# A gated hybrid layer on one core: the modulation vectors computed from unsplit fp32 weights in two column groups of TensorE

## The chip, the cores and the metric

The kernel runs on one core of a Trainium2 chip. A core has TensorE (PE, matrix products and transposes into PSUM), VectorE (DVE), ScalarE (ACT), GpSimd (POOL), and SyncE (SP), whose queue issues all DMA transfers of this kernel. The metric is the device time of one execution in microseconds; the median of three runs of the kernel before is 1617.76 us (1617.69 to 1618.45).

## The reference

The layer takes 1024 latent tokens and 256 context tokens of width 1024. Each token is RMS-normalised and modulated, and the result is multiplied by a large input matrix `w_in`; two branches (a gated linear attention, GLA, and a differential attention) follow, then gates, an output projection and a residual. The part that matters here is the modulation:

```python
mod_x = jax.nn.silu(c) @ w_ada[layer] + b_ada[layer]
mod_c = jax.nn.silu(c_ctx) @ w_ada[layer] + b_ada[layer]
sh_x, sc_x, g_x = jnp.split(mod_x[:, None, :], 3, axis=-1)
sh_c, sc_c, g_c = jnp.split(mod_c, 3, axis=-1)
pl = project(modulate(x, sh_x, sc_x), w_in[layer])      # rms_norm(x) * (1 + scale) + shift
pc = project(modulate(ctx, sh_c, sc_c), w_in[layer])
```

So two vectors (latent and context) of 1024 are multiplied by the first 2048 columns of `w_ada` (8 MB in fp32) before any token can be modulated. The third part, `g_x`, is needed only where `w_out` is prepared. Everything is fp32, and the results must keep fp32 accuracy.

## The kernel before

A large product is made of three fp32r products: each operand is split into a high part (a ScalarE copy into fp32r) and a low part (a VectorE subtraction), and `mm3` issues high by high, high by low and low by high. One such product of 128 x 128 by 128 x 512 is one TensorE record in the trace.

The kernel writes out the order of work on PE, ScalarE, VectorE and GpSimd itself. Tasks are Python generators; `Driver` (line 59) keeps a modelled clock for each engine, and a task that yields is taken up again at the modelled time at which its data are there, the lowest `prio` first. `At(70.0)` is a modelled time of that clock. What is emitted first stands first in the engine's queue, and the engines take their queues in order, so an instruction whose data are late holds up all behind it. Tiles come from pools with fixed numbers of slots (`TAGS`, line 235 on; `w` has 18, `p` 5, `pl` 4, `raw` 3, `l5` 3, `x2` 5, `x4` 1, `g5` 6; the PSUM banks are `mm` 3, `tp` 2, `gs`, `go`, `gt` 1 each); `acq` waits for a free slot, `rel` gives it back.

The first stretch is `prologue` (line 505). `consts` loads the two vectors, makes their SiLU and transposes them into the columns `col`. `loads` (532) then issues the transfers: for each of eight blocks `k` of 128 rows the first half of the modulation weights (512 columns of shift and 512 of scale, two tiles of `w`), between them the first four token tiles (`XL`, line 680, says behind which block), then two blocks of `w_in`, then the second half. Token tiles are normalised by `xnorm`.

`ada(part)` (583) makes the products of a half. In the first half it is plain fp32: the two columns of `col` are the stationary operand, 512 columns of weights stream past, and shift and scale go to the banks `gs` and `go`. In the second half the weights go into `raw` and `l5` slots, `conv` (566) splits them into high and low parts in slots of `w` and `pl`, and the products are fp32r: four stationary columns (`cs`: high and low of both vectors) against the high weights and two against the low ones. At the end of a half ScalarE copies one bank and VectorE the other into SBUF, eight small transposes bring them into columns (bank `gt`), and VectorE adds the bias: `shsc[part]`, the shift and scale of four of the eight row blocks of tokens. `ev_sh[part]` says that they are there.

The end of `prologue` transposes the tokens: for each of the eight row blocks four transposes into a `tp` bank, and `hblock` (640) applies shift and scale on ScalarE, makes the high part on GpSimd and the low part on VectorE. The loop waits for `ev_sh` before it transposes a block.

`wstream` (686) loads and splits the blocks of `w_in`. Its first two transfers (`RAWS`) may go behind the first half, the others behind the second; the split of the later ones waits for the event `ev_wc`, which `conv` sets at its end, as do the token tiles 4 to 9. `job` (741) makes the products of one group of weights, for one group of output blocks after the other: the first group has `G0` = 3 blocks in the three `mm` banks (3 blocks x 8 k x 3 products), the next ones a single block. For the first weights, the GLA keys, `post_gk` copies the result out and releases `mm`.

`job_gate` (762) computes `g_x` on VectorE from the rest of `w_ada`: eight transfers of 512 KB, one after the other through the one slot `x4`, two operations each, a PE product with ones per half, and at the end the event `ev_gbt`. It is started at the modelled time 70. The pair weights (943) use `x4` too, and `presums` (1045) needs `ev_gbt` to prepare `w_out`; the GLA stage opens (`to_gla`, 1277) when `presums` has ended.

Of the kernel before, what the change touches and what calls it, by code (L numbers as in the profile page):

```python
# [232 lines left out]
class Hybrid:  # L233
# [27 lines left out]
    def __init__(self, tc, nc, a, out):  # L261
        self.tc, self.nc, self.a, self.out = tc, nc, a, out
        self.n, self.ny, self.ng, self.ys = 0, 0, 0, {}
        self.d = d = Driver()
        self.act, self.dve, self.pool = Engine(d, "ACT", nc.scalar), Engine(d, "DVE", nc.vector), Engine(d, "POOL", nc.gpsimd)
        self.free, self.freed = {}, {}
        self.pools = {}
        self.recent = []

# [78 lines left out]
    def mm(self, out, lhsT, rhs, start, stop, more=False):  # L348
        self.ins = self.nc.tensor.matmul(out, lhsT, rhs, start=start, stop=stop, skip_group_check=more).ins  # L349
# [76 lines left out]
    def consts(self):  # L426
# [78 lines left out]
    def prologue(self):  # L505
# [21 lines left out]
        ev_w = {(k, part): Event() for k in range(NK) for part in range(2)}  # L527
        ev_r = [Event() for _ in range(NK)]
        ev_sh = [Event(), Event()]
        shsc = [self.c(f"shsc{x}", [P, 2, 4, 2]) for x in range(2)]  # L530

        def loads():

            for part in range(2):
                for k in range(NK):
# [23 lines left out]
            d.set(self.ev_wl[1])  # L559
            yield self.ev_wc  # L560
            for i in range(4, 10):
# [3 lines left out]

        def conv():
            for k in range(NK):
                yield ev_r[k]
                tg, raw = ev_r[k].raw
                ev, tw = ev_w[k, 1], ("w", "pl")[k % 2]  # L570
                yield from self.acq(tw, 4)
                ev.w = []
                for s in range(2):
                    hi = self.t(tw, [P, 512], F32R)
                    lo = self.t(tw, [P, 512], F32R)
                    yield self.act.activation(hi, raw[:, s], AF.Copy)
                    e = (self.pool if s in self.CP else self.dve).tensor_tensor(lo, raw[:, s], hi.bitcast(F32), ALU.subtract)
                    ev.w.append((hi, lo))
                self.rel(tg, e)
                d.set(ev, e)  # L580
            d.set(self.ev_wc)

        def ada(part):


            m = 4 if part else 2
            pa = []
            for tg in ("gs", "go"):
                yield from self.acq(tg)
                pa.append(self.t(tg, [m, 512]))  # L590
            for k in range(NK):
                yield ev_w[k, part]
                for x, w in enumerate(ev_w[k, part].w):
                    if part:

                        prods = [(pa[x], self.cs[:, k], w[0]), (pa[x][:2], self.cs[:, k, :2], w[1])][::-1 if k else 1]
                        for y, (o, c, ww) in enumerate(prods):
                            e = self.mm(o, c, ww, k == 0 and y == 0, k == NK - 1 and y == 1)
                    else:
                        e = self.mm(pa[x], self.col[:, k:k + 9:8], w, k == 0, k == NK - 1)  # L600
                        self.rel("w", e)
                        yield AtPE(0)
                if part:
                    self.rel(("w", "pl")[k % 2], e, 4)
                    yield AtPE(0)
            md = []
            for x, tg in enumerate(("gs", "go")):
                yield from self.acq("p")
                md.append(self.t("p", [m, 512]))
                if x:  # L610
                    e = self.dve.tensor_copy(md[x], pa[x])
                else:
                    e = self.act.activation(md[x], pa[x], AF.Copy)
                self.rel(tg, e)
            if part == 0:
                d.spawn(ada(1), prio=-1)
            yield from self.acq("gt")
            pt = self.t("gt", [P, 2, 4, m])
            for x in range(2):
                yield d.whenpe(md[x])  # L620
                for y in range(4):
                    e = self.tr(pt[:, x, y], md[x][:, y * P:(y + 1) * P])
                self.rel("p", e)
            yield self.d.when(pt)
            ss = shsc[part]
            for x in range(2):
                o = 24 + 8 * x + 4 * part
                e = self.dve.scalar_tensor_tensor(ss[:, x], pt[:, x, :, 0:2], float(x), self.col[
                    :, o:o + 4].unsqueeze(2).to_broadcast([P, 4, 2]), ALU.add, ALU.add)
            if part:  # L630
                e = self.dve.tensor_tensor(ss, ss, pt[:, :, :, 2:4], ALU.add)
            self.rel("gt", e)
            d.set(ev_sh[part], e)

        yield from self.consts()
        self.d.spawn(loads(), prio=-2)
        self.d.spawn(conv(), prio=-2)
# [28 lines left out]
        for half in (0, 1, 2):  # L666
# [3 lines left out]
            for k in range(NK):  # L670
                yield ev_sh[k // 4]
                yield from self.acq("tp")
# [6 lines left out]

    XL = ({1: (0,), 2: (1,), 4: (2,), 6: (3,)}, {})  # L680
    RAWS = 2
    CP = ()
    G0, NG = 3, 2


    def wstream(self, jobs, tag, gate=None, prio=3, after=()):

        queue = [(n, src, c0, kk) for n, (src, c0) in enumerate(jobs) for kk in range(NK // 2)]
        wd = Weights({(n, k): Event() for n in range(len(jobs)) for k in range(NK)})
        loaded = [Event() for _ in queue]  # L690

        def load():
            for ev in after[:1]:
                yield ev
            for x, (n, src, c0, kk) in enumerate(queue):
                if gate and x in (0, self.RAWS):
# [4 lines left out]
                self.d.set(loaded[x], self.dma(raw, src[kk * 256:(kk + 1) * 256, c0:c0 + 512].rearrange(  # L701
                    "(k p) c -> p k c", p=P)))

        def run():
            for ev in after[1:]:
                yield ev
            for x, (n, src, c0, kk) in enumerate(queue):
                yield loaded[x]
                if gate and x == self.RAWS:
                    yield gate[2]  # L710
# [30 lines left out]
    def job(self, wd, n, items, width, mms, post, wtag, ptag="mm", first=1, last=2):  # L741

        gs = self.groups(items, first, last)
# [86 lines left out]
    def phase_a(self):  # L830
# [35 lines left out]

        self.ev_wl, self.ev_wc = [Event() for _ in range(2)], Event()
        wd = self.wstream([(self.win, j[0]) for j in jobs], "w", (*self.ev_wl, self.ev_wc))
        self.wload = wd.loaded
        self.ev_pl, self.ev_pw, self.ev_zl = Event(), Event(), Event()  # L870
# [538 lines left out]
    def post_gk(self, s, half, pm):  # L1409
        o, n = self.hspan(half)  # L1410
        yield from self.acq("p")
        st = self.t("p", [P, n])
        self.rel("mm", self.act.activation(st, pm, AF.Copy))
        self.store([(self.d_k[s][:, o:o + n], st)], ("p", 1))
# [1396 lines left out]
```

## Time and profile before

| | before |
|---|---|
| median of three runs | 1617.76 us |
| span of the profiled execution | 1614.1 us |
| PE busy | 1591.4 us (99%) |
| VectorE, ScalarE, GpSimd busy | 1224.4, 835.7, 634.3 us |
| first `w_in` product on PE | 27.90 us |
| granted TensorE clock | 1.00 in all slices |

The time of the profiled execution itself is not given; its span, from the first to the last instruction, is 3.66 us shorter than the median of the timed runs, and what lies around the span is in the timed runs only. In a row of a view, L349 is the helper that issues all matmuls, L375 the one for transposes, L201 the one for all work on ScalarE, VectorE and GpSimd, L314 the one for transfers; so groups are told apart by tiles (`out<-in`). `PEld` are weight loads, which overlap with matmuls. The modelled ends of matmuls overlap too; the spacing of their starts is what they cost in a row. Times in views are us from the start of the span.

### The profile page before, as it was taken

The numbers are of one execution on the slowest core, as the hardware profiler recorded it, in microseconds if no ns is written. First come the engines' busy times: TensorE is split into PE (matmuls) and PEld (weight loads), VectorE is DVE, ScalarE is ACT, GpSimd is POOL, SyncE is SP. The second block draws the span as 40 slices with busy tenths as digits, with TensorE's granted clock in tenths as the row PEclk, the third lists the DMA queues.
The fourth block names the chain that finished last, engine by engine and source line by source line (L and its number), as shares of the span: only waits on it lengthen the run. The fifth ranks groups of instructions, "written<-read, shape, count | busy, mean of one in ns | idle before, by whom it ended". The sixth has DMA issues, their size and how long they took to land.

```text
span 1614.1 us, 24349 instructions
## 1 busy us (share of the span) xinstructions
PE 1591.4 (99%) x8229; PEld 1328.1 (82%) x8229; DVE 1224.4 (76%) x2118; ACT 835.7 (52%) x1720; POOL 634.3 (39%) x663
## 2 busy tenths in 40 slices
PE   8999999999999999999999999999999999999999
PEld 3788888888888888888888788888888888888887
DVE  4787945676777779767677688878778888888994
ACT  4776523435343454555535566665665666656331
POOL 1500000001415667535564256656765666560000
PEclk9999999999999999999999999999999999999999
DMA  8576996998878367564645944545587545347662
GB/s 305 201 257 239 329 304 232 344 331 295 278 238 281 116 194 235 167 212 118 189 118 158 253 121 121 151 129 151 150 264 218 159 137 150 111 155 285 204 206 100
DMA packets 259565, 331.16 MB, mean 205 GB/s; under 512 B 22600, under 2 KB 160752, under 8 KB 259440
## 3 DMA queue, kind: packets, MB, share of 16 engines
q1 hardware_dynamic: 259440, 329.60, 63.8%
q8 instruction: 65, 1.06, 0.3%
q14 instruction: 60, 0.49, 0.1%
HBM read 225.20 MB, written 104.33 MB: 204 GB/s over the span
## 4 chain that ended last, share of the span: by engine, by line
PE 89%; DVE 4%; issue 2%; DMA 2%; ACT 1%; POOL 1%; SPq 0%; ACTq 0%; DVEq 0%; POOLq 0%
PE mm L349 30%; PE mb L349 11%; PE s L349 8%; PE mc L349 7%; PE b L349 6%; PE tp L349 5%; PE gt L349 5%; PE b L375 5%; PE go L349 4%; PE gs L349 4%; PE mz L349 2%; PE tp L375 2%; DVE sm L201 1%; POOL at L201 1%; DMA w<-in_w_ada 1%
## 5 line engine op out<-in xcount | busy, mean ns | idle before, releaser
L349 PE MATMUL mm<-w,h 128*128 128x512 f32 x912 | 231.0, 400 | 0.0
L349 PE MATMUL mb<-h,wt 128*128 128x512 f32 x840 | 223.0, 400 | 0.0
L201 DVE TENSOR_REDUCE sm<-s 128x1 f32<-128x1024 f32 (+1 forms) x192 | 193.3, 1037 | 10.7 <-PE s L349 6.6
L201 ACT ACTIVATE e<-s,sm 128x1280 f32<-128x1280 f32 x128 | 169.3, 1329 | 54.4 <-DVE sm L201 51.2
L349 PEld LDWEIGHTS mm<-w,h 128*128 128x128 f32 x912 | 167.4, 188 | 32.8
L201 POOL TENSOR_TENSOR at<-ac,at 128x512 fp32r<-128x512 f32 x128 | 188.2, 1471 | 10.7
L349 PEld LDWEIGHTS mb<-h,wt 128*128 128x128 f32 x840 | 151.4, 188 | 28.6 <-DVE ft L201 0.3
L201 POOL TENSOR_SCALAR at<-ac 128x512 fp32r<-128x512 f32 x128 | 96.9, 757 | 191.0 <-ACT ac L201 190.7
L349 PE MATMUL s<-hk,aq 128*128 128x512 f32 x744 | 169.0, 363 | 1.9 <-ACT e L201 1.8
L349 PE MATMUL mm<-h,w 128*128 128x512 f32 x672 | 168.2, 400 | 1.0 <-DVE h L201 1.0
L349 PEld LDWEIGHTS mm<-h,w 128*128 128x128 f32 x672 | 123.7, 188 | 26.4 <-DVE h L201 1.5
L201 DVE TENSOR_TENSOR w<-raw,w 128x512 fp32r<-128x512 f32 x128 | 96.0, 766 | 54.2 <-ACT w L201 52.0
L349 PEld LDWEIGHTS s<-hk,aq 128*128 128x128 f32 x744 | 117.7, 189 | 18.5 <-ACT e L201 3.6
L349 PE MATMUL b<-at,vv 128*128 128x256 f32 x960 | 130.1, 287 | 1.1 <-ACT ac L201 0.8
L349 PEld LDWEIGHTS b<-at,vv 128*128 128x128 f32 x960 | 119.5, 191 | 2.8 <-ACT ac L201 1.0
L201 ACT ACTIVATE w<-raw 128x512 fp32r<-128x512 f32 x128 | 78.1, 626 | 84.2 <-PE tp L349 23.8
L201 ACT ACTIVATE ac<-b 128x512 f32<-128x512 f32 x122 | 72.5, 598 | 91.8 <-PE b L375 91.7
L201 POOL TENSOR_TENSOR sm<-sm,nhalf 128x2 f32<-128x2 f32 (+2 forms) x94 | 107.7, 1146 | 27.9 <-DVE sm L201 22.7
L201 DVE SCALAR_TENSOR_TENSOR e<-e,sm,e 128x1280 f32<-128x1280 f32 x64 | 117.9, 1842 | 1.0
L349 PE MATMUL mm<-w,g 128*128 128x512 f32 x432 | 105.7, 389 | 0.0
L349 PEld LDWEIGHTS mm<-w,g 128*128 128x128 f32 x432 | 81.1, 188 | 16.9
L375 PE MATMUL b<-ident,e 128*128 128x128 f32 x610 | 92.6, 273 | 1.3 <-ACT ac L201 0.8
(357 smaller groups left out, 3054.2 us busy)
## 6 DMA issues: line engine op xcount, KB each, us to landing
raw<-in_w_in SPq DMA_DIRECT2D x62, 512.0 KB, 4.3
g<-d_s SPq DMA_DIRECT2D x32, 640.0 KB, 6.2
g<-d_s SPq DMA_DIRECT2D x32, 512.0 KB, 5.7
aq<-d_qT SPq DMA_DIRECT2D x124, 128.0 KB, 3.4
d_dv<-pl SPq DMA_DIRECT2D x40, 256.0 KB, 3.9
gv<-d_v SPq DMA_DIRECT2D x40, 256.0 KB, 3.3
d_kT<-pl SPq DMA_DIRECT2D x40, 256.0 KB, 2.8
hk<-d_kT SPq DMA_DIRECT2D x32, 320.0 KB, 5.9
```

The lines of the kernel that those rows point to most:

```text
L201: self.ins = f(out, *args, **kw).ins
L349: self.ins = self.nc.tensor.matmul(out, lhsT, rhs, start=start, stop=stop, skip_group_check=more).ins
L375: self.nc.tensor.transpose(out, src, self.ident[:n, :n])
```

## The change

In both halves a product is now plain fp32 from the loaded weights. The stationary operand `cols` has 32 columns (two vectors, the rest zeros); shift uses column group 0 of TensorE and partitions 0 to 31 of one PSUM bank, scale group 1 and partitions 32 to 63. The second half has the bank `go` and its transposes a `tp` bank. `conv` and `cs` are gone; the second half's weights go to slots of `l5`, `pl`, `x2` and `w` that are free at that time, and two blocks of `w_in` are issued before token tiles 4 to 9. The first group of products has four blocks, the fourth in the bank `gt`. The tokens' transposes stand ahead of the wait for `ev_sh` (up to the two `tp` banks), and the token tiles 2 and 3 are loaded one block earlier. `job_gate` starts at the modelled time 160. `wd.issued` is set when a transfer is issued, not when it has landed.

```diff
+    def mmc(self, out, lhsT, rhs, x, start, stop):
+        out = out[32 * x:32 * x + 32]
+        self.ins = self.nc.tensor.matmul(out, lhsT, rhs, start=start, stop=stop, tile_position=(0, 32 * x)).ins
+        return self.d.op("PE", 0.43, [out], [lhsT, rhs])
...
+        self.cols = self.c("cols", [P, NK, 32])
+        self.pool.memset(self.cols, 0.0)
...
-        self.cs = self.c("cs", [P, NK, 4], F32R)
-        for x in range(2):
-            c = self.col[:, x * 8:x * 8 + 8]
-            self.dve.tensor_copy(self.cs[:, :, x], c)
-            self.dve.tensor_tensor(self.cs[:, :, 2 + x], c, self.cs[:, :, x].bitcast(F32), ALU.subtract)
+        self.dve.tensor_copy(self.cols[:, :, 0:2], self.col[:, 0:16].rearrange("p (s k) -> p k s", s=2))
...
-                        tg = ("l5", "raw")[k % 2]
-                        yield from self.acq(tg)
-                        raw = self.t(tg, [P, 2, 512])
-                        self.dma(raw, src)
-                        ev_r[k].raw = tg, raw
-                        d.set(ev_r[k], d.when(raw))
+                        tg = th[k]
+                        n = 1 if tg == "l5" else 2
+                        yield from self.acq(tg, n)
...
+                        d.set(ev, d.when(*ev.w))
...
             d.set(self.ev_wl[1])
-            yield self.ev_wc
+            for x in range(self.RAWS, NK // 2):
+                yield self.wload[x]
             for i in range(4, 10):
...
-        def conv():
...
+        th = ("l5", "l5", "l5", "pl", "pl", "x2", "x2", "w")
...
+            tb = ("gs", "go")[part]
+            yield from self.acq(tb)
+            pa = self.t(tb, [64, 512])
             for k in range(NK):
                 yield ev_w[k, part]
+                if part and k % 2 == 0:
+                    yield ev_w[k + 1, part]
                 for x, w in enumerate(ev_w[k, part].w):
-                    if part:
...
+                    e = self.mmc(pa, self.cols[:, k], w, x, k == 0, k == NK - 1)
...
+            yield from self.acq("p")
+            md = self.t("p", [64, 512])
+            self.act.activation(md[:, :256], pa[:, :256], AF.Copy)
+            e = self.dve.tensor_copy(md[:, 256:], pa[:, 256:])
+            self.rel(tb, e)
...
+            for y in range(4):
+                e = self.tr(pt[:, y], md[:, y * P:(y + 1) * P])
...
         def hblock(k, half, pt):
...
+            yield ev_sh[k // 4]
             yield from self.acq("p")
...
             for k in range(NK):
-                yield ev_sh[k // 4]
+                if k == 4:
+                    yield ev_sh[1]
                 yield from self.acq("tp")
...
-    XL = ({1: (0,), 2: (1,), 4: (2,), 6: (3,)}, {})
+    XL = ({1: (0,), 2: (1,), 3: (2,), 5: (3,)}, {})
     RAWS = 2
-    CP = ()
-    G0, NG = 3, 2
+    G0 = 4
...
+                    if gate:
+                        yield self.d.on("ACT", raw)
...
-            for it in g:
-                yield from self.acq(ptag)
-                pms.append(self.t(ptag, [P, 512]))
+            for x, it in enumerate(g):
+                tg = "gt" if ptag == "mm" and x == 3 else ptag
+                if x == 3:
+                    yield self.ev_sh[0]
+                yield from self.acq(tg)
+                pms.append(self.t(tg, [P, 512]))
+                self.bank[d.key(pms[-1])] = tg
...
-        d.spawn(self.job_gate(), At(70.0), prio=4)
+        d.spawn(self.job_gate(), At(160.0), prio=4)
```

More of the change, by code (lines that the diff above doesn't have):

```diff
@@ L267, in __init__ @@
         self.pools = {}
-        self.recent = []
+        self.recent, self.bank = [], {}
     def open(self, *names):
@@ L527, in prologue @@
         ev_w = {(k, part): Event() for k in range(NK) for part in range(2)}
-        ev_r = [Event() for _ in range(NK)]
-        ev_sh = [Event(), Event()]
+        ev_sh = self.ev_sh
         shsc = [self.c(f"shsc{x}", [P, 2, 4, 2]) for x in range(2)]
@@ L544, in loads @@
                     else:
-                        tg = ("l5", "raw")[k % 2]
-                        yield from self.acq(tg)
-                        raw = self.t(tg, [P, 2, 512])
-                        self.dma(raw, src)
-                        ev_r[k].raw = tg, raw
-                        d.set(ev_r[k], d.when(raw))
+                        tg = th[k]
+                        n = 1 if tg == "l5" else 2
+                        yield from self.acq(tg, n)
+                        if n == 1:
+                            raw = self.t(tg, [P, 2, 512])
+                            self.dma(raw, src)
+                            ev.w = [raw[:, x] for x in range(2)]
+                        else:
+                            ev.w = [self.t(tg, [P, 640 if tg == "x2" else 512])[:, :512] for _ in range(2)]
+                            for x in range(2):
+                                self.dma(ev.w[x], src[:, x])
+                        d.set(ev, d.when(*ev.w))
                     for i in self.XL[part].get(k, ()):
@@ L564, in loads @@
                 self.d.spawn(xnorm(i))
-        def conv():
[L567 to L581, printed above, removed]
@@ L603, in ada @@
                 if part:
-                    self.rel(("w", "pl")[k % 2], e, 4)
+                    self.rel(th[k], e, 1 if th[k] == "l5" else 2)
+                else:
+                    self.rel("w", e, 2)
+                if part == 0 or k % 2:
                     yield AtPE(0)
[L606 to L614, printed above, removed]
+            yield from self.acq("p")
@@ L615, in ada @@
+            md = self.t("p", [64, 512])
+            self.act.activation(md[:, :256], pa[:, :256], AF.Copy)
+            e = self.dve.tensor_copy(md[:, 256:], pa[:, 256:])
+            self.rel(tb, e)
             if part == 0:
                 d.spawn(ada(1), prio=-1)
[L617 to L623, printed above, removed]
+            tb = ("gt", "tp")[part]
@@ L624, in ada @@
+            yield from self.acq(tb)
+            pt = self.t(tb, [P, 4, 64])
+            yield d.whenpe(md)
+            for y in range(4):
+                e = self.tr(pt[:, y], md[:, y * P:(y + 1) * P])
+            self.rel("p", e)
             yield self.d.when(pt)
@@ L627, in ada @@
                 o = 24 + 8 * x + 4 * part
-                e = self.dve.scalar_tensor_tensor(ss[:, x], pt[:, x, :, 0:2], float(x), self.col[
+                e = self.dve.scalar_tensor_tensor(ss[:, x], pt[:, :, 32 * x:32 * x + 2], float(x), self.col[
                     :, o:o + 4].unsqueeze(2).to_broadcast([P, 4, 2]), ALU.add, ALU.add)
-            if part:
-                e = self.dve.tensor_tensor(ss, ss, pt[:, :, :, 2:4], ALU.add)
-            self.rel("gt", e)
+            self.rel(tb, e)
             d.set(ev_sh[part], e)
@@ L689, in wstream @@
         wd = Weights({(n, k): Event() for n in range(len(jobs)) for k in range(NK)})
-        loaded = [Event() for _ in queue]
+        loaded, wd.issued = ([Event() for _ in queue] for _ in range(2))
         def load():
@@ L702, in load @@
                     "(k p) c -> p k c", p=P)))
+                self.d.set(wd.issued[x])
         def run():
@@ L741, in job @@
     def job(self, wd, n, items, width, mms, post, wtag, ptag="mm", first=1, last=2):
-        gs = self.groups(items, first, last)
+        d, gs = self.d, self.groups(items, first, last)
         for g in gs:
             pms = []
-            for it in g:
-                yield from self.acq(ptag)
-                pms.append(self.t(ptag, [P, 512]))
+            for x, it in enumerate(g):
[5 more added lines that the diff above has]
+                self.bank[d.key(pms[-1])] = tg
             for k in range(NK):
@@ L864, in phase_a @@
         self.fill_from = 4 + self.NS
-        self.ev_wl, self.ev_wc = [Event() for _ in range(2)], Event()
-        wd = self.wstream([(self.win, j[0]) for j in jobs], "w", (*self.ev_wl, self.ev_wc))
-        self.wload = wd.loaded
+        self.ev_wl, self.ev_sh = ([Event() for _ in range(2)] for _ in range(2))
+        wd = self.wstream([(self.win, j[0]) for j in jobs], "w", self.ev_wl)
+        self.wload = wd.issued
         self.ev_pl, self.ev_pw, self.ev_zl = Event(), Event(), Event()
```

17 lines of the change are left out of this document (1 added, 16 removed).

## The prediction

> **What bounds the kernel now.** I read the page first, then what TensorE (PE) waits for in two windows, then the chain of waits and PE's timeline through the first 60 us, because every edit but one lies there.
>
> ```profile
> span 1614.1 us, 24349 instructions
> PE 1591.4 (99%) x8229; PEld 1328.1 (82%) x8229; DVE 1224.4 (76%) x2118; ACT 835.7 (52%) x1720; POOL 634.3 (39%) x663
> ```
>
> PE is busy for nearly all of the span, so only PE work that disappears, or PE idleness that is filled, can move the end. The waits of PE, first up to 60 us, then from 60 us to the end (its longest row):
>
> ```profile
> PE tp L375 <- ACT p L201: 2.3, 2, 1.3
> PE gt L375 <- DVE p L201: 1.2, 2, 0.7
> PE mm L349 <- DVE h L201: 1.0, 1, 1.0
> ```
> ```profile
> PE s L349 <- ACT e L201: 2.0, 3, 1.3
> ```
>
> After 60 us the largest wait is 2.0 us in 1550: the rest of the kernel is a fixed amount of PE work, and it ends earlier by as much as it is reached earlier. So the forecast is made at one landmark, the moment at which 72 products of the first group (`mm`, three blocks of 8 k with 3 products) and the 32 transposes of the first 512 tokens are done. The chain of waits (start, us, what) shows it:
>
> ```profile
> 10.94 6.61 DMA w<-in_w_ada
> 17.54 0.02 issue
> 17.56 7.36 DMA raw<-in_w_in
> ...
> 26.00 0.77 ACT p L201
> ...
> 28.14 4.27 PE mm L349 x18
> 32.41 0.47 PE gs L349 x2
> ...
> 35.10 0.60 PE go L349 x2
> 35.70 2.74 PE mm L349 x12
> 38.45 0.47 PE gs L349 x2
> ...
> 40.30 1.39 PE mm L349 x6
> 41.69 0.24 PE gs L349
> ...
> 45.12 0.60 DVE p L201
> ...
> 46.17 1.04 PE tp L375 x8
> ...
> 50.98 8.25 PE mm L349 x35
> 59.23 0.88 PE tp L375 x8
> ```
>
> The landmark is 59.23. Up to 17.5 us the chain is the load of the first half's weights, then two blocks of `w_in`. From 28.14 PE works; 35 + 18 + 12 + 6 products are in these rows and one more lies before 50.98, so 72 products take 8.25 + 4.27 + 2.74 + 1.39 + 0.23 = 16.9 us. Between them the 32 products of the second half (`gs`, `go`) take 3.29 (32.41 to 35.70), 1.85 (38.45 to 40.30) and, twelve at 0.235, 2.8 us: 7.9 in all. From 41.69 the chain leaves PE: ScalarE and VectorE convert the last weights, copy the sums out, and make the next normalised blocks. Of 50.98 - 41.69 = 9.29 us PE works 2.8 (the twelve), 1.76 (16 transposes, 0.88 for eight), 0.8 (the eight small transposes, below) and 0.23: 3.7 us are lost.
>
> **The change part by part.**
>
> *First half in two column groups.* Before, each fp32 product is two matmul records, on PE's timeline:
>
> ```profile
> 5.73 1.87 PE L349 MATMUL gs<-w,col 128*2 128x512 f32 x2 [0.29 <-DVE col L201]
> 7.39 1.91 PE L349 MATMUL go<-w,col 128*2 128x512 f32 x2
> ...
> 11.99 1.02 PE L349 MATMUL gs<-w,col 128*2 128x512 f32 x2
> 12.85 1.02 PE L349 MATMUL go<-w,col 128*2 128x512 f32 x2
> ...
> 21.58 1.02 PE L349 MATMUL gs<-w,col 128*2 128x512 f32 x2 [0.40 <-DMA w<-in_w_ada]
> 22.43 1.02 PE L349 MATMUL go<-w,col 128*2 128x512 f32 x2
> ```
>
> One costs 0.86 us (12.85 - 11.99), two records 0.43 apart. The first cost 1.66 (7.39 - 5.73): PE starts at half pace, though the granted clock reads 1.00. At 21.58 PE waits for the transfer of the last block, so the weights set the end here and faster products gain little: the last `go` could start when its weights are there, at most 0.86 earlier.
>
> *Out of PSUM and transposed.* One 64-row bank takes the place of two, read half by ScalarE, half by VectorE, and four small transposes take the place of eight. Groups of the first 60 us (count | busy, mean ns):
>
> ```profile
> L201 ACT ACTIVATE p<-tp,shsc 128x512 f32<-128x512 f32 x8 | 5.9, 769 | 0.1
> ...
> L375 PE MATMUL gt<-ident,p 2*128 2x2 f32 (+1 forms) x16 | 1.6, 202 | 1.3 <-DVE p L201 1.2
> ...
> L201 DVE COPY p<-go 2x512 f32<-2x512 f32 (+1 forms) x2 | 1.3, 671 | 0.0
> ...
> L201 ACT ACTIVATE p<-gs 2x512 f32<-2x512 f32 (+1 forms) x2 | 1.2, 581 | 0.6 <-PE gs L349 0.6
> ```
>
> Four transposes are 0.4 us, eight 0.8. Half copies are about half of 0.58 and 0.67 plus a fixed part; side by side they save 0.3, one after the other they cost as much as now. The first eight big transposes (two `tp` banks) now stand ahead of the wait for the scales; PE idles there, so that costs nothing, and without that cover it would be 0.88. The block at 26.00 (`p<-tp`, 0.77) then waits for the scales alone. With the copy and the transposes its start moves by 0 (ScalarE still busy with the second `w_in` block, which it splits until 26.00) to 1.1 (it goes first, as the scales come at about 24.9). I take 0.8: products from 27.3 on.
>
> *Second half without split.* Gone are 16 copies on ScalarE and 16 subtractions on VectorE and the wait for slots. Added are 16 fp32 products. If the two column groups ran in full side by side, they would cost 8 x 0.86 = 6.8; in turns 16 x 0.86 = 13.7. I take a value between: the two records of one product use the same columns and must follow each other, so that in program order only the second record of group 0 can run with the first of group 1. A pair alone then takes 3 x 0.43 = 1.28, two pairs in a row, as the change issues them, 5 x 0.43 = 2.14, four such groups 8.6. That is 0.7 more than the 7.9 of now: PE does not gain from the column groups, it only doesn't lose.
>
> The Trainium skill's "TensorE: Matmul & The Clock Gate", Part 3, says that column tiles overlap (2.38x for three) while matmuls stay in program order: the first half is what I assume, the second is the stagger; no run here shows either. Its page "TensorEngine Tiling (Array Packing)", section Key Properties, speaks against the change: a switch of tiling mode drains the array. The nearest row is the tail of one record, 0.592 long (below) at a spacing of 0.43; ten switches at 0.16 would bring 8.6 to 10.2 and the gain from 4.1 to 2.5.
>
> ```profile
> L349 PE MATMUL gs<-w,col x16: 592/592/1061, 5.7 to 22.0; 128*2 128x512 f32 x16
> ```
>
> *Places of its own.* The loads need not wait for conversions. The transfers up to 32 us and two 1 us stretches:
>
> ```profile
> DMA packets 5116, 10.48 MB, mean 327 GB/s; under 512 B 482, under 2 KB 522, under 8 KB 5116
> ```
> ```profile
> 30.00:31.00 1.00, 1.00 (x6) 0.83 (x5) 1.00 (x2) 1.00 (x3) 0.27 (x1) 1.00 1.06 399
> ...
> 32.00:33.00 1.00, 1.00 (x6) 0.34 (x4) 1.00 (x3) 0.14 (x1) 0.00 (x0) 1.00 0.08 29
> ```
>
> Blocks and token tiles are 0.524 MB each; 10.48 MB are 20 of them: eight of the first half, four of tokens, two of `w_in`, six of the second half. At 32 us two are missing and the DMA falls idle, for want of slots. Without that the last two (1.05 MB at 0.39 MB/us) are there at 35 to 36. From there the scales and the first new block need 1.3 (pair) + 1.0 (copies) + 0.4 + 0.3 + 0.9 (transposes) + 0.8 + 0.6 + 0.7, so it is ready near 42.
>
> *Four blocks at a time* (`G0` 4, the fourth in bank `gt`). That is the cover: until the second half's scales come, PE has 4 x 4 x 3 = 48 products, 11.3 us, and the 8.6 of the second half: from 27.3 until 47.2. Ready at 42 against 47.2 leaves 5 us, so of the 3.7 us lost I keep 0.2 (0 to 0.7). With three blocks it would be 36 products and the cover would end at 44.3. The tokens' transfers, 3.1 MB that now come behind two `w_in` blocks, end near 46; PE needs them only behind the first group.
>
> *The gate's weights at 160 instead of 70.* 16 VectorE operations and 4 MB leave a stretch in which PE waits for nothing and go to another one; I count 0. What could make it cost is under the rivals.
>
> **Sum.** Products from 27.3; + 16.9 + 1.8 (16 transposes) + 0.4 + 8.6 + 0.2 = 55.2 at the landmark, against 59.2: 4.1 us earlier with rounding left out. The span would go from 1614.1 to 1610.0. The page's execution has 3.7 us around its span if it took the median, 1617.76; I carry the difference over to the median: 1613.7. The own range of this case: 1611.5 (6.8 for the products, 1.1 and no stall: 6.3 earlier) to 1616.3 (10.2, start 0.3 earlier, stall 0.7: 1.4 earlier).
>
> **The rivals.**
>
> *Column groups take turns.* Nothing in this trace shows two products at once; for it speaks only that they use other columns. Second half 13.7, and the first half's last product, behind its partner as now, starts the group 0.3 later than forecast: 27.6 + 16.9 + 1.8 + 0.4 + 13.7 + 0.2 = 60.6, 1.4 later: 1619.2. If the weight loads, 0.085 each, also lay open for all 32 records, 2.7 more: 1621.9. This is the slower side; it decides as soon as the second half costs more than 12.3.
>
> *The gain is given back later.* Behind the landmark some chain on other engines may not move up with PE, say the sums of tokens that go through HBM and are needed from 189 on. Against it: PE waits nowhere in that stretch, and VectorE is relieved by the gate's work. Then 1617.8.
>
> *The gate comes too late.* The fence shows SP's queue and the gate's end:
>
> ```profile
> 214.18 0.38 SPq L314 DMA_DIRECT2D x<-in_w_ada  x1
> ...
> 222.99 0.39 SPq L314 DMA_DIRECT2D x<-in_w_ada  x1
> ...
> 240.63 0.38 SPq L314 DMA_DIRECT2D x<-in_w_in  x1
> ...
> 285.30 0.81 SPq L314 DMA_DIRECT2D l<-in_w_out  x2
> ```
> ```profile
> L201 POOL TENSOR_SCALAR gb<-p x2: 617/806/994, 115.3 to 245.7; 128x512 f32<-128x512 f32 x2
> ```
>
> Its one slot `x4` is also used by the pair weights, until 214 and from 240.63 to 285. Blocks take some 8 us (222.99 - 214.18), so three or four fit before and the other half after 285; the gate would be there near 325, not 246, and the two sums of `w_out` that begin at 285.30 come 40 us late. If they don't catch up before the GLA stage opens, PE lacks its filler: 10 us, 1623.7 or so.
>
> *Half pace again.* With its products paired PE is busy for perhaps 60% of the first half. If it falls back to the pace of 5.73, some 5 us of the first group run at half: 2.5 lost, 1616.2. The gaps are one transfer long (1.3 us) and PE has kept its pace over a wait of 1.3.
>
> **How the numbers follow.** The forecast 0.62, turns 0.16, given back 0.12, gate late 0.05, half pace 0.05. No change is within 0.2%, 3.2 us: 1614.5 to 1621.0. Of the forecast's 0.62 about 0.50 lies below 1614.5, and 0.03 of the others' does: faster 0.53. Slower than 1621.0 are the gate and a third of the turns: 0.10. The rest, 0.37, is no change. For 8 in 10 the range runs from 1611.0 to 1619.5.
>
> **What would show it.** Right: pairs of `gs` or `go` records of the two groups that overlap in time, two pairs in about 2.1 us; no PE wait over 0.5 us between 28 and 55; the last `w_ada` block of the second half landed by 36; the first transposes ahead of the small ones; the landmark (96 products now, so at 55.2 + 24 x 0.235 = 60.8 for the whole group of four) 4 us earlier; the same 4 us at the first score product. Wrong: 0.86 between starts of the two groups; PE waits on `h` before 47; PE waits between 160 and 200 or before the scores; or a first group at 0.46 per product.

## The result and the profile after

The changed kernel takes 1626.16 us (median of 4 runs, 1625.0 to 1628.97) against 1617.72 for the kernel before in the same comparison: ratio 1.0055, 95% interval 1.0041 to 1.0070. It is slower by 8.4 us where 4.1 us less were forecast. The profiled execution took 1628.97 us, the slowest of the four, with a span of 1627.0. Two executions of later runs, one of e2 (2673 us) and one of e10 (3235 us), fell into a slow state and are left out of every median and ratio here.

The head of the page of the changed kernel:

```profile
span 1627.0 us, 24307 instructions
...
PE 1602.4 (98%) x8221; PEld 1328.5 (82%) x8221; DVE 1213.9 (75%) x2098; ACT 824.4 (51%) x1704; POOL 632.8 (39%) x664
```

VectorE and ScalarE have less to do, as the change says (1224.4 and 835.7 before). PE has eight instructions fewer, and yet it is busy for 11.0 us more than the 1591.4 of before. So most of the loss is not new waiting: PE works longer on the same products. (Two stretches at half clock, shown below, are part of the 11.0 in this execution, 1.7 us each.) From 60 us on its longest waits are still short; the first row is new:

```profile
PE tp L380 <- ACT p L201: 1.9, 2, 1.0
PE s L349 <- ACT e L201: 1.8, 2, 1.3
```

The groups of all instructions (count | busy, mean ns of one) show which products are longer. Before, then after:

```profile
L349 PE MATMUL mb<-h,wt 128*128 128x512 f32 x840 | 223.0, 400 | 0.0
L349 PE MATMUL mm<-w,g 128*128 128x512 f32 x432 | 105.7, 389 | 0.0
```
```profile
L349 PE MATMUL mb<-h,wt 128*128 128x512 f32 x840 | 224.8, 402 | 0.0
L349 PE MATMUL mm<-w,g 128*128 128x512 f32 x432 | 108.3, 395 | 0.0
```

A record of `mm<-w,g` (products in the second stage of the pairs; `mm` is the bank) is 6 ns longer. The records overlap, so length alone is not cost; PE's timeline shows that the pace is slower too. The same nine products, before and after:

```profile
189.02 2.20 PE L349 MATMUL mm<-w,g 128*128 128x512 f32 x9
191.06 0.84 PE L349 MATMUL gs<-w,g 128*128 128x512 f32 x3
```
```profile
190.21 2.26 PE L349 MATMUL mm<-w,g 128*128 128x512 f32 x9
192.31 0.85 PE L349 MATMUL gs<-w,g 128*128 128x512 f32 x3
```

Nine take 2.04 us before (191.06 - 189.02) and 2.10 after: 226.7 and 233 ns for each. The change edits nothing there. There are 864 products `w,g` in all banks together; 6 ns each are 5 us, and the `h,wt` above add 1.8 (224.8 - 223.0). Products whose operands are both on the left have kept their pace: twelve `w,h` in a row take 2.72 us, 226.7 ns each, in the changed kernel too (366.34 to 369.06).

The chain of waits through the first 60 us, after (start, us, what):

```profile
18.86 7.03 DMA raw<-in_w_in
...
26.97 0.77 ACT p L201
...
28.89 2.96 PE go L356 x8
...
33.84 1.84 PE go L356 x8
```

Eight records are two pairs of fp32 products, and the second half has four such groups. Three of them take 1.84 us each; the first one takes 2.96, because PE ran at half clock. In the windows of the changed kernel (stretch; busy time of the five engines; granted clock; DMA):

```profile
25.00:30.00 5.00, 3.00 (x16) 1.56 (x16) 3.87 (x9) 4.08 (x7) 1.96 (x3) 0.77 1.04 402
30.00:35.00 5.00, 5.00 (x22) 2.00 (x20) 1.76 (x3) 0.78 (x1) 1.47 (x2) 0.89 1.05 405
...
75.00:80.00 5.00, 4.38 (x21) 3.62 (x22) 2.70 (x5) 3.38 (x7) 2.50 (x6) 0.66 0.00 0
```

0.77 and 0.89 over 5 us each are 3.4 us at a clock of 0.5 (2 x 5 x (0.23 + 0.11)), and so is 0.66. So each stretch costs 1.7 us of work. Before, the clock was 1.00 in these windows. But this belongs to the execution and not to the change: two of the four timed executions have a mean clock of 1.000 and still take 1625.28 and 1625.00.

Where the time goes, by landmarks (start of the instruction named, us; in brackets the difference to before). The 72 products of the forecast's landmark end at 57.3, 1.9 earlier than the 59.2 of before; the first product of the second stage of the pairs starts at 190.21 (+1.2), the GLA stage at 535.19 (+9.1), the first score product at 919.91 (+8.9), the last product at 1622.81 (+12.8). The time is lost in two stretches: 7.9 between the second stage of the pairs and the GLA stage, where the products `w,g` are, and 3.9 behind the first score product, where most of the products `h,wt` are. 0.86 of the 7.9 is only moved: the gate's first product on PE, two records, stood ahead of this stretch (109.44) and now stands in it (260.43).

The differences at the end are larger than the 8.4 us of the medians, because the two profiled executions are not alike. The one after is the slowest of its four. For the one before, 1614.1 is the span; every execution whose span is on record took 1.7 to 2.1 us more than its span, so this one took about 1616, near the fastest of the kernel before (1616.08) and not its median.

### The profile page after: what moved, and what is told of

Same layout as the page of the kernel before. It is cut to its first block, busy times and chain, and to the rows that moved or that the text cites. A ratio compares the mean times of both kernels' runs of the same rounds, so it can differ in the third digit from the quotient of the medians.

```text
span 1627.0 us, 24307 instructions
## 1 busy us (share of the span) xinstructions
PE 1602.4 (98%) x8221; PEld 1328.5 (82%) x8221; DVE 1213.9 (75%) x2098; ACT 824.4 (51%) x1704; POOL 632.8 (39%) x664
## 4 chain that ended last, share of the span: by engine, by line
PE 88%; DVE 5%; ACT 2%; DMA 2%; POOL 1%; issue 1%; SPq 0%; ACTq 0%; DVEq 0%; POOLq 0%
PE mm L349 29%; PE mb L349 11%; PE s L349 8%; PE mc L349 7%; PE b L349 6%; PE tp L349 6%; PE gt L349 5%; PE b L380 5%; PE go L349 4%; PE gs L349 4%; PE mz L349 2%; PE tp L380 2%; DVE sm L201 1%; DMA w<-in_w_ada 1%; POOL at L201 1%
## 5 line engine op out<-in xcount | busy, mean ns | idle before, releaser
L349 PE MATMUL mb<-h,wt 128*128 128x512 f32 x840 | 224.8, 402 | 0.0
L349 PE MATMUL mm<-h,w 128*128 128x512 f32 x648 | 162.8, 399 | 0.0
L349 PEld LDWEIGHTS mm<-h,w 128*128 128x128 f32 x648 | 119.1, 188 | 24.7 <-issue 1.7
```

## The experiments

"e1" and so on name the runs; all were timed in five rounds beside the kernel before, whose median was 1617.3 to 1617.9. The second number in each result is the ratio to it with its 95% interval. A ratio and a quotient of medians can differ by 0.1%, so differences below some 2 us between runs say little. Where PE's landmarks are compared, they come from one profiled execution of each run.

### e1 and e2: the place of the tiles

`cols` takes 1024 bytes of each partition, and `cs`, which it replaces, took 128. The constants lie at the left end of SBUF, so all pools that open on the left (`w`, `h0`, `h1`, `p`, `pl`, `raw`, `hk`) have moved up by 896 bytes; the pools on the right (`g5`, and later `wt`) stayed. In the compiled program the first `w` tile starts at byte 111232 of a partition before and at 112128 after, the first `g5` tile at 162176 in both. e1 is the changed kernel with 128 unused bytes more, e2 the kernel before with 896.

```diff
 # e1, in the changed kernel
+        self.c("pad", [P, 32])
 # e2, in the kernel before
+        self.c("pad", [P, 224])
```

> The changed kernel with 128 bytes of unused constants more, so that all tiles behind the constants lie 1024 bytes higher than in the kernel before instead of 896. Theory A (the place of the tiles slows products whose two operands lie on different sides of the on-chip memory): products of the groups w,g return from 232 to 227 ns apart, the stretch from the first pair product to the first score product from 742 to 734 us, and the time falls from 1626 to 1616 to 1619. Theory B (the loss comes from the new order of work, the place has no effect): 1625 to 1628, spacing stays 232.

> The kernel before with 896 bytes of unused constants and no other edit, so that its tiles lie where those of the changed kernel lie. Theory A: it becomes 7 to 12 us slower, 1625 to 1630, with products w,g at 232 ns. Theory B: 1617.7 as before.

e1: 1618.54 us, 1.0001 (0.9992 to 1.0009). e2: 1626.63 us, 1.0051 (1.0037 to 1.0064). The group of `mm<-w,g`, first e1, then e2:

```profile
L349 PE MATMUL mm<-w,g 128*128 128x512 f32 x432 | 106.0, 389 | 0.0
```
```profile
L349 PE MATMUL mm<-w,g 128*128 128x512 f32 x432 | 108.2, 395 | 0.0
```

The 896 bytes alone make the kernel before 9.1 us slower, and 128 bytes more take 7.6 us off the changed one. So the loss is a by-product of the place, and the change proper, with that taken out, is worth nothing measurable: e1 equals the kernel before within 0.1%.

### e5: the same cure from the other side

```diff
-    EDGE = 96
+    EDGE = 224
```

> The changed kernel, with the spare tile at the right end of SBUF 128 bytes per partition larger, so that every tile of the right side lies 128 bytes lower and the left side stays where the change put it. If the pace of a product depends on how its two operands lie to one another, the distance between left and right is again that of the kernel before (modulo 1024: 640 to 384 then, 512 to 256 now), and products of a w tile with a g tile are 226.7 ns apart as in e1: 1617 to 1621 us. If the absolute place of the w tiles (512 modulo 1024) is what counts, they stay at 232 ns and the time at 1624 to 1628.

1617.73 us, 1.0000 (0.9991 to 1.0009); the row of `mm<-w,g` is that of e1 (106.0, 389). Here the `w` tiles lie where the change put them, and the `g5` tiles 128 bytes lower. The distance from the first `w` tile to the first `g5` tile is 50944 before, 50048 in the changed kernel and in e2, 49920 in e1 and e5. All `w` tiles lie multiples of 1024 bytes apart, all `g5` tiles too, so modulo 1024 the distance is the same for every pair of them: 768, 896 and 768. The same place of `w` was slow (changed kernel) and fast (e5), and the same place of `g5` too (changed kernel, e1): it is the distance of the two operands that counts, not the place of either. Only these two distances were measured, so no rule follows for others, and why 896 is slower than 768 no run shows.

### e9: the column groups undone

e9 is e1 with both products of a pair in one column group; the second one has a PSUM bank of its own, and each engine copies out one bank of 512 columns in place of half a bank.

```diff
-        out = out[32 * x:32 * x + 32]
-        self.ins = self.nc.tensor.matmul(out, lhsT, rhs, start=start, stop=stop, tile_position=(0, 32 * x)).ins
+        self.ins = self.nc.tensor.matmul(out, lhsT, rhs, start=start, stop=stop, tile_position=(0, 0)).ins
...
-                    e = self.mmc(pa, self.cols[:, k], w, x, k == 0, k == NK - 1)
+                    e = self.mmc((pa, pb)[x], self.cols[:, k], w, x, k == 0, k == NK - 1)
```

> e1 with the fp32 products of the weights of both halves in one column group of TensorE, the second product of each pair in a bank of its own, so that nothing runs side by side; all else of the change stays. By e1's trace a pair of products costs 0.86 us and two pairs 1.84; in turns two pairs would be 4 x 0.86 = 3.44, four such groups 13.8 in place of 7.4, so the group of four ends 6.4 us later than in e1 if PE is the bound there. Theory (the column groups carry the early gain, and PE bounds this stretch): pairs of halves start near 166, and the end is 3 to 6 us later than e1's, 1622 to 1625. Rival (what is gained there is waited away behind the group anyway): the waits at 71 to 74 shrink, pairs start near 162 and the end is 1618 to 1620.

1622.39 us, 1.0038 (1.0025 to 1.0052), 3.9 us more than e1 by the medians and 6 by the ratios. PE's timeline in e9, and in e1:

```profile
32.85 1.04 PE L355 MATMUL go<-l,cols 128*32 128x512 f32 x2
33.73 1.02 PE L355 MATMUL gs<-l,cols 128*32 128x512 f32 x2
34.59 1.02 PE L355 MATMUL go<-pl,cols 128*32 128x512 f32 x2
35.45 1.02 PE L355 MATMUL gs<-pl,cols 128*32 128x512 f32 x2
36.40 0.97 PE L349 MATMUL mm<-h,w 128*128 128x512 f32 x3
```
```profile
31.53 1.05 PE L356 MATMUL go<-l,cols 128*32 128x512 f32 x4
32.41 1.03 PE L356 MATMUL go<-pl,cols 128*32 128x512 f32 x4
33.37 0.96 PE L349 MATMUL mm<-h,w 128*128 128x512 f32 x3
```

Two pairs take 3.55 us in turns and 1.84 in two column groups: a pair costs what one product costs, 0.86 to 0.88, and some 0.1 is lost where PE goes over to 128-column products. In the records the two products of a pair start 7 ns apart.

### e3: three blocks in place of four

```diff
-    G0 = 4
+    G0 = 3
```

(in e1)

> As e1_pad128, with three blocks in the first group instead of four. Theory C (the fourth block was the work that covers the making of the second and third token blocks between 60 and 80 us): the PE waits and the half clock between 65 and 80 us disappear and the time is 2 to 4 us below e1_pad128. Rival (the group of four is needed until the second half's scales are there): PE waits of 2 to 5 us appear between 40 and 50 us and the time is not below e1_pad128.

1622.78 us, 1.0030 (1.0019 to 1.0041). The waits of e1 at 71 to 74 (shown in the next section) are gone, but from 60 to 200 PE now waits for the split of `w_in`:

```profile
PE mm L349 <- DVE w L201: 2.5, 2, 1.4
PE mm L349 <- DVE pl L201: 1.0, 1, 1.0
```

The fourth block is worth 4.2 us in e1. These rows account for 3.5, and this execution has a half-clock stretch at 165 besides; that PE, with a fourth block for each pair of weights, leaves VectorE the time to keep ahead is how I read them.

### e6 and e8: what the fourth block costs

In e1 the gain is 4.2 us at the landmark (55.04 against 59.2) and 2.0 at the second stage of the pairs. Between them lie two waits in PE's timeline, and the queue of SP tells why:

```profile
71.06 0.44 PE L380 MATMUL tp<-ident,g 128*128 128x128 f32 x2 [1.00 <-ACT p L201]
...
73.37 0.90 PE L380 MATMUL tp<-ident,g 128*128 128x128 f32 x4 [0.94 <-ACT p L201]
```
```profile
63.38 4.58 SPq L314 DMA_DIRECT2D l<-in_gla_w_decay  x8
68.48 14.10 SPq L314 DMA_DIRECT2D d_k<-p  x5
```
```profile
65.19 0.78 ACT L201 ACTIVATE p<-tp,shsc 128x512 f32<-128x512 f32 x1 [0.41 <-DVE h L201]
67.49 0.78 ACT L201 ACTIVATE p<-tp,shsc 128x512 f32<-128x512 f32 x1 [1.52 <-DVE h L201]
...
70.23 0.78 ACT L201 ACTIVATE p<-tp,shsc 128x512 f32<-128x512 f32 x1 [1.48 <-DVE h L201]
```

The four blocks of products are copied out into four of the five `p` slots at 62.7 to 64.8. Their stores stand behind eight loads of the decay weights and start at 68.48; until then one slot is left, and ScalarE (last fence) makes one normalised block, then waits until VectorE is done with it. e6 issues the loads behind the stores; e8 has the gate at 110 as well, e7 the gate alone, all in e1.

```diff
 # e6 and e8
+        self.d.set(self.ev_plr, self.d.when(*ws))
+        yield At(68.0)
         self.dve.memset(dw, 0.0)
         for r in range(4):
             for e in range(2):
                 self.dma(dw[r * 32 + e * 16:r * 32 + e * 16 + 16, e * 512:(e + 1) * 512], a["gla_w_decay"][0, e])
...
+        self.d.set(self.ev_dw, self.d.when(dw))
...
+                yield self.ev_dw
...
 # e7 and e8
-        d.spawn(self.job_gate(), At(160.0), prio=4)
+        d.spawn(self.job_gate(), At(110.0), prio=4)
```

> e1 with the eight loads of the decay weights issued some 8 us later (at 68 in the order's own time), behind the stores of k. Theory: in e1 PE's waits of 1.00 and 0.94 us at 71.06 and 73.37 come from the five p slots; four are held by the drained k blocks, whose stores stand behind those eight loads in SP's queue from 63.4 to 68.5, so that ScalarE makes one normalised block at a time. Then the stores go out near 64 to 66, the two waits are gone and the pairs of halves start some 2 us earlier than in e1 (159.8): near 158. Rival: ScalarE, GpSimd and VectorE are the bound of these blocks themselves; then the waits stay. At the end: 1616.6 if nothing takes the 2 us away, 1618.5 if the stretch behind 160 does.

> e1 with the gate's weights at 110 in place of 160 (70 was tried: 1626.5). By the theory that the gate's late second product and the late sums of w_out cost 3 us behind 160 in e1, an earlier gate has its second product before 300 and the first product of the GLA stage no later than 526.1, as in the kernel before; the end then near 1616. If each move of the gate lays out the engines' queues anew, with waits elsewhere, as at 70, the time is 1619 to 1626.

> e6 and e7 together: the loads of the decay weights behind the stores of k, and the gate's weights at 110. If both gains are kept: 1614 to 1615, faster than both kernels. If the gate's place only exchanges one wait for another: as e7 or slower.

e6: 1618.53 us, 1.0004 (0.9996 to 1.0013). e7: 1619.39, 1.0008 (1.0000 to 1.0017). e8: 1617.07, 0.9997 (0.9988 to 1.0005). In e6 and e8 both waits on `p` are gone, as the theory says, but PE waits 1.7 and 1.9 us for the decay rates instead: the memset came late in VectorE's order, so the loads left at 77.47 and 76.04 (63.38 in e1). The one row of PE's waits in e6 from 60 to 200 us:

```profile
PE gs L349 <- DVE l L201: 1.7, 1, 1.7
```

e7 shows no gain from the gate at 110. Only one of its eight blocks came earlier by it, because `x4` was taken by the pairs' weights.

### e10, e11, e12: both waits away, and the gain still lost

e10 is e8 with the loads at 62, e11 the same with the gate at 85, e12 is e8 with the memset in its old place.

> e8 with the loads of the decay weights at 62 instead of 68: in e8 they went out so late that PE waited 1.9 us for the decay rates' inputs (l on VectorE), in e6 1.7. At 62 they should go out behind the stores of k and be there in time: that wait gone, the pairs of halves near 157, the end 1.5 to 2 us before e8's, 1615.2 (1614 to 1616.5). If they stand before the stores again, the waits on p at 71 to 74 come back and the time is 1617 to 1619.

> As the one before with the gate's weights at 85 in place of 110: four of its eight blocks then stand ahead of the pairs' weights in SP's queue and four between 210 and 245, as in the kernel before, so that the sums of w_out are loaded before 310 and PE's waits of 0.4 to 0.9 us between 370 and 435 go: 2 us less from 338 to 526. If these waits are what the late gate costs: 1613 to 1615. If the early gate lays ScalarE's queue out anew, with waits for w between 100 and 180 as the gate at 70 did in e4 (4.16 and 1.35 us): 1617 to 1622.

> e8 with the memset of the decay weights' tile where it was in e1 and only seven of its eight loads behind the stores of k (in e8 the memset stood among VectorE's work at 75, so that the loads left at 76 and PE waited 1.9 us at 84.6; in e10, at 62, loads and memset both stood ahead again and the waits on p came back). If the five p slots are the cause of the waits at 71 to 74 and the late loads of the one at 84.6, neither is there: the pairs of halves start near 157.2, 4.6 us before the kernel before, and the end is 1.9 us before e8's, 1615.2: faster than both kernels by 0.15%. If the clock falls to half in a stretch where PE is partly idle, up to 1.7 us are lost for each such stretch: 1617 to 1619.

e10: 1618.80 us, 1.0007 (0.9997 to 1.0016); e11: 1619.51, 1.0011 (1.0002 to 1.0020). In both the loads went out ahead of the stores again and the two waits on `p` were back. e12: 1619.55, 1.0014 (1.0005 to 1.0023), against my expectation of 1615.2. There the head does what was forecast: the view of PE's waits is empty from 60 to 330, and the second stage of the pairs starts at 184.57, 4.45 us earlier than before. But the GLA stage starts at 528.84, 2.7 later than before. PE's waits from 330 to 530 in e12:

```profile
PE gs L349 <- ACT p L201: 2.3, 1, 2.3
PE tp L349 <- DMA g<-d_s: 1.3, 1, 1.3
PE mm L349 <- DVE w L201: 1.1, 1, 1.1
```

They sum to 5.4 us with two small ones (0.7), against 1.3 before, and in 376 to 380 the granted clock falls to 0.64, a half-clock stretch that costs 1.7 more.

### e4, e13, e14: the place of the gate in the queue

In e12 three of the gate's eight blocks stand behind the first loads of `w_out` in SP's queue, and `presums` cannot use these before the gate is there:

```profile
225.20 0.45 SPq L314 DMA_DIRECT2D x<-in_w_ada  x1
280.86 0.80 SPq L314 DMA_DIRECT2D l<-in_w_out  x2
282.07 0.38 SPq L314 DMA_DIRECT2D x<-in_w_ada  x1
...
295.73 0.38 SPq L314 DMA_DIRECT2D x<-in_w_ada  x1
```

In the changed kernel and in e1 it is four, and the gate's second product on PE stands at 325.43 in the changed kernel and 319.82 in e1 (242.07 before, 307.18 in e12, 253.85 in e13). e13 is e12 with the gate at 85, e14 with the gate at 70, e4 is e1 with the gate at 70; in e13 and e14 all eight blocks stand ahead of `w_out`.

```diff
 # e13, against e12
-        d.spawn(self.job_gate(), At(110.0), prio=4)
+        d.spawn(self.job_gate(), At(85.0), prio=4)
```

> As e1_pad128, with the gate's work started at the modelled 70 again. If moving the gate cost nothing, as the forecast said: within 1 us of e1_pad128. If the late gate costs (sums of w_out late, later stage late): 2 us or more below e1_pad128. If moving it helped: above e1_pad128.

> e12 with the gate at 85 in place of 110: three more of its blocks are loaded ahead of the pairs, and all eight stand ahead of w_out in SP's queue, as in the kernel before. Theory (the late gate gives the gain back): the waits of 2.35, 1.09 and 1.3 us between 375 and 400 are gone, the group of sums at 339.5 before is at 335 here and the GLA stage starts some 4 us earlier than before, at 522: 1613.5. Rival (the engines' orders behind 340 give it back in any case): the GLA stage starts at 525 or later, 1617 to 1620.

> e12 with the gate at 70, the time of the kernel before; its blocks too are all ahead of w_out. If what cost e4 8 us (ScalarE's queue at 114 to 125 with three table loads in front of w) depends on the order that the rest leaves, it need not come back: 1613.5 as for 85. If the gate at 70 costs it in any new order, PE waits on w between 100 and 180 and the time is 1618 to 1626.

e13: 1615.73 us, 0.9989 (0.9980 to 0.9998): 0.11% less than the kernel before. It is the only one of fourteen runs whose interval lies below 1, and only just, so part of this can be chance. e14: 1626.79, 1.0052 (1.0040 to 1.0065). e4: 1626.52, 1.0051 (1.0037 to 1.0065). In e13 the last load of the gate leaves at 237.55, the first of `w_out` at 283.38, and from 330 to 530 PE waits 2.3 us in place of 5.4:

```profile
PE gs L349 <- ACT p L201: 1.4, 1, 1.4
PE gt L349 <- DVE p L201: 0.6, 1, 0.6
PE tp L349 <- DVE p L201: 0.3, 1, 0.3
```

The landmarks side by side (start of the instruction, us; in brackets the difference to before):

| | gate's first product | second stage of the pairs | GLA stage | last product |
|---|---|---|---|---|
| before | 109.44 | 189.02 | 526.10 | 1610.02 |
| e1 | 255.68 | 187.00 (-2.0) | 527.49 (+1.4) | 1611.60 (+1.6) |
| e12 | 229.46 | 184.57 (-4.45) | 528.84 (+2.7) | 1612.45 (+2.4) |
| e13 | 125.80 | 185.88 (-3.1) | 525.19 (-0.9) | 1608.67 (-1.4) |

Between the second stage and the GLA stage e12 loses 7.2 us and e13 2.2. Of the 7.2, 0.86 is the gate's first product, which is only moved into this stretch, and 1.7 the half clock; the waits are 4.1 more than before. In e13 they are 1.0 more, and 0.8 is a wait at 238.75; the rest of the 2.2 is not settled. So moving the gate from 110 to 85 takes away most of what e12 lost. It is not a price that holds in every order: e10 and e11 differ by the same move, the stretch is 2.7 shorter in e11 (338.39 against 341.07, 0.86 of it moved), and yet e11 is not faster (1619.51 against 1618.80). That the gate's blocks behind `w_out` are the link is read from the queue; with a new start time the order of the other engines changes too.

The gate at 70 costs 8.0 us in e4 (against e1) and 11.1 in e14 (against e13), by ScalarE's queue. In e4 PE's timeline and ScalarE's:

```profile
125.27 9.98 PE L349 MATMUL mm<-h,w 128*128 128x512 f32 x30 [4.16 <-ACT w L201]
```
```profile
114.74 1.28 ACT L201 ACT_TABLE_LOAD   x1
116.03 2.44 ACT L201 ACTIVATE g<-g 128x1280 f32<-128x1280 f32 x2
118.49 1.28 ACT L201 ACT_TABLE_LOAD   x1
119.78 2.43 ACT L201 ACTIVATE g<-g 128x1280 f32<-128x1280 f32 x2
122.12 1.06 ACT L201 ACTIVATE p<-mm 128x512 f32<-128x512 f32 x2
123.20 1.28 ACT L201 ACT_TABLE_LOAD   x1
...
124.60 1.66 ACT L201 ACTIVATE w<-raw 128x512 fp32r<-128x512 f32 x3
```

The split of the next weights stands behind three table loads, two passes over the decay rates (`g<-g`) and a copy, 9.9 us in a row. In e14 PE waits for splits of `w` too, 3.4 us for ScalarE's part between 100 and 180 and 2.6 for VectorE's:

```profile
PE mm L349 <- ACT w L201: 3.4, 2, 2.2
```

With the gate at 85 (e13) the order written out is another, and from 60 to 200 PE waits 0.4 us in all. The idle stretch in e4 is followed by 6.8 us at half clock (the windows 125 to 130 and 130 to 135 read 0.50 and 0.85), 3.4 us more.

## Why the prediction was wrong

**The step that failed.** "After 60 us the largest wait is 2.0 us in 1550: the rest of the kernel is a fixed amount of PE work, and it ends earlier by as much as it is reached earlier." The work was not fixed: its pace changed with the place of the tiles. And little waiting was not a sign of room: a gain at the landmark could be lost again in new waits behind it. The step failed in three ways. The first is shown by e1, e2 and e5; of the other two the waits are shown, and their prices are those of single orders.

- *Place.* In the list of parts `cols` does not occur as memory. It takes 896 bytes more than `cs`, and these cost 7.6 us (changed kernel against e1) to 9.1 (e2 against before). No rival held it. Within the noise this is the whole of the 8.4 us.
- *The cover was paid for with slots.* "Four blocks at a time" was costed by its banks only. Its four copies take four of the five `p` slots behind a queue of loads: two waits of 1.94 us together in e1, gone in e6, e8 and e12. In e6 and e8 another wait of 1.7 to 1.9 takes their place; only in e12 and e13 is PE rid of both.
- *The gate.* The 16 operations and 4 MB "leave a stretch in which PE waits for nothing and go to another one; I count 0." From the second stage of the pairs to the GLA stage e1 loses 3.4 us (0.86 of it moved, 1.7 in waits beyond those of before, the rest open) and e12 7.2; with the gate's loads in the place of before (e13) it is 2.2. The rival "the gate comes too late" had the mechanism and the moment ("near 325", measured 325.43), but a price of 10 us and a chance of 0.05. Setting the time back to 70 costs 8. The step had treated a modelled start time as a small shift; it is an input of the whole written order.

Of the prediction's own signs, "the same 4 us at the first score product" showed it: that product came 8.9 later, not 4 earlier.

**The landmark was nearly right, in part by luck.** It was forecast at 55.2. In e1 the 72nd product starts at 54.81, so the landmark is at 55.04, 4.2 earlier than before. In the changed kernel's profiled execution it is at 57.3; 2.3 more are a later start and the half clock there. That e1 hits to 0.2 us is luck in part: two terms below are off by -1.2 and +0.8 and cancel. The whole group of four was forecast at 60.8; in e1 its last product ends at 62.28, with 16 transposes of later tokens (1.76) among it: 60.5. Of the terms:

- The second half, 8.6, was 7.4 (4 x 1.84). The assumed stagger ("only the second record of group 0 can run with the first of group 1") is not there; both records of a pair run side by side. The upper bound, 13.7 in turns, was 14.2 in e9.
- "Products from 27.3": 29.96 in e1, of which 1.84 are two pairs that the order put ahead; so 0.8 late. In the changed kernel 32.20: in that execution the transfers are 1.3 later (18.86 against 17.56; e5, with the same instructions, has 17.36), and the pairs ran at half clock.
- The cover held: no wait of PE over 0.5 us between 32 and 60, and the scales' transposes stood at 43.37 in the changed kernel, 40.74 in e13 (forecast 42 for the block behind them).
- The tokens' transfers "end near 46": two are issued at 33.06, the other four only from 49.65 on, as before (49.48), because `g5` has six slots and these are freed by the transposes of the first tokens. PE needed them only at 60.
- The 3.7 us that the sum puts around the span are 1.7 to 2.1 in all executions on record. The forecast of the difference doesn't depend on it.

**The rivals.** Turns (0.16): fell by the trace, and e9 prices it: the 72nd product starts at 61.25 in place of 54.81, 6.4 later, and the end is 3.9 (medians) to 6 us (ratios) later. Some is made up behind the landmark, where the waits on `p` shrink from 1.94 to 1.2 when PE comes later. Given back later (0.12, 1617.8): this is the time of e1, 1618.54, but mostly by other chains than the one it names; the sums that go through HBM are one row of e1 (`tp<-` waits 0.7 us for `g<-d_s`). Half pace again (0.05): it came in the profiled execution, at 28 and again at 75, 3.4 us each, and it did not in e1, where PE was as idle in 25 to 30 (2.91 of 5 us busy, 3.00 in the changed kernel). The last section shows what differs. It is no part of the 8.4 us, since executions at full clock have the loss too.

## What to carry to other kernels

A new constant moves every tile behind it; where the time changes and no wait does, compare the mean of one record of the same group in both profiles, and try a pad of the size that puts the old distance back. In a kernel where PE is busy nearly all the time, a gain at the head can be lost again behind it, as here: look at the queues of all engines and at the slots, not only at the waits that PE has now. Where an order is laid out by a model, a start time is not a shift, and two or three values have to be tried.

## What the runs showed of the hardware

- The pace of a product of 128 x 128 by 128 x 512 depends on how its operands lie to one another in SBUF: 226.7 ns apart where `w` and `g5` tiles lie 768 bytes apart modulo 1024, 232 to 233 where it is 896. The kernel before and e2 differ in nothing but the unused constant.
- Two fp32 products of 128 x 32 by 128 x 512 in two column groups cost what one costs (0.86 to 0.88 us), and start 7 ns apart.
- The granted clock falls to half for 3.413 us (28 and 75 in the changed kernel, 377 in e12) or twice that (125 in e4). In an execution with several falls these start on a common beat: 27.70 and 75.49 in the changed kernel, 47.79 or 14 x 3.413 apart; 29.07, 124.64 and 175.84 in e4, 28 and 15 beats apart. The beat lies elsewhere in each execution. In the changed kernel the interval before the fall, 24.29 to 27.70, holds nearly the whole wait at 27.78 (2.00 us; PE busy 1.49 of 3.41 us); in e1 the beat cuts the same stretch in two, 2.03 and 2.69 busy, and the clock stays. How much idle time it takes stays open: an interval of 2.02 busy was followed by a fall in e2 (23.23 to 26.64), one of 1.53 was not in e3 (25.36 to 28.77).
